# Hybrid decoder step: the products with the memory move onto units of the first output projection, the samples' rows onto score units

## Chip, core and metric

One core of a Trainium2 chip runs the whole step. The metric is the device time of one execution in microseconds (us). The kernel before takes 3266.39 us (median of three runs, 3266.05 to 3266.45).

## The reference, cut to what matters

One layer of a causal decoder runs on a prompt of 2048 tokens and on 8 samples of one token each; the width is 1024. The mixers (dilated attention and sliding-window attention) give `oa` and `ob`, which are normalised, joined and sent through `w_out`. Then comes the part that the change is about, attention to 256 memory tokens, with 4 heads of 256:

```
x = x + mixers_out(oa, ob, ...)            # ... @ w_out
k, v = split(rms_norm(mem, g_mem) @ w_mem_kv)     # memory keys and values of the prompt
q = (rms_norm(x, g_cross) @ w_xq) per head
p = softmax(q @ k.T / 16);  o = p @ v
x = x + o @ w_xo
x = x + conv_ffn(rms_norm(x, g_ffn))
```

The samples go through the same layer with memory keys and values of their own, which are inputs. All data are float32.

## The kernel before, in words

**Two halves of a product.** TensorE multiplies in a reduced float32 format, so every operand is split into a rounded part and a remainder ("hi" and "lo"; `hi_of` and `lo_of`, lines 108 to 121): ScalarE writes hi, VectorE (for some GpSimd) writes lo. Each product takes three matmuls: hi by hi, lo by hi, hi by lo.

**The weight stream.** `WStream` (line 127) holds a list of weight blocks, called units, each 512 KB, in the order in which they are used. A unit is loaded by the DMA queue of the SyncE (SP) into one of three raw tiles `wr`, split into one of four pairs `wh`, `wl`, and handed out by `get()`. `ahead(n)` writes the splits of the next n units into the program; each split also writes the loads of the next units. A unit marked whole is not split: `get_whole()` hands out the raw tile. In the kernel before the splitting stops at a whole unit until that has been handed out.

**Order of the work.** The program is written as one sequence per engine. A planner then lists each engine's instructions by a simulated time line: it keeps the written order as priority, and moves an instruction ahead where its inputs and a buffer are free. On the chip each engine, and each DMA queue, then works through its own list in order.

**The memory products.** Instead of computing queries, the kernel multiplies the weights with the memory once: for each head h, `qk_d` holds `w_xq` times the head's keys, and `vo_d` the head's values times `w_xo`. This is the block of lines 1674 to 1731, between the mixers and the output projection. For each head `mem_panel` loads keys or values (tile `kv`, split into `mkv`), `mem_q` takes a whole unit of `w_xq`, transposes it on TensorE (line 1695, 8 transposes; the result is split into `wT`) and multiplies (line 1708, 24 matmuls of 256 columns), and `mem_o` multiplies one split unit of `w_xo` (line 1721, 12 matmuls of 512 columns). Each runs twice a head. The sums lie in PSUM banks of the ring `g`, with four buffers; `store_w` copies them out (tile `az`; ScalarE for `mem_q`, VectorE for `mem_o`) and stores them to `qk_d` and `vo_d` in device memory.

**The chunks.** After that come four chunks of 512 tokens; `pre(c, ...)` (line 1282) does the part before the feed-forward, `ffn` the rest. In `pre`:
- `gemm_full(oT, ...)` multiplies the joined mixer outputs by `w_out`: 8 units, 24 matmuls of 512 columns each (lines 887 to 889); `ev_out` adds and splits each finished block.
- `scores(h)` (line 1311) multiplies by `qk_d` for head h: 2 units of 48 matmuls of 256 columns (line 1319), then the softmax; `transp` turns the softmax for the next product.
- chunk 2 takes the 8 samples along (`s_in`); after the four heads `sample_rows` (line 1357) multiplies the samples' rows, kept in `las`, by `w_xq`: 8 units of 8 matmuls of 256 columns (line 1368). Chunk 3 (`s_out`) does the same with `w_xo`, to take the samples' attention back in.
- `gemm_two` and `gemm_full` multiply by `vo_d`.

After each unit `tick()` runs one queued side task; every fourth tick issues a copy of 1 MB of the cache.

PSUM has eight banks: two in the ring `a` (`bankA`: all transposes, `sample_rows`, sums for the norms), two in `s` (scores of even heads), four in `g`.

The order of the block before `pre` is:

```
    for h in range(4):
        mk = mem_panel(h)
        for hf in range(2):
            mem_q(h, hf, mk)
        mv = mem_panel(4 + h)
        for hf in range(2):
            mem_o(h, hf, mv)
```

Of the kernel before, what the change touches and what calls it, by code (L numbers as in the profile page):

```python
# [8 lines left out]
F32 = mybir.dt.float32  # L9
# [4 lines left out]
ALU = mybir.AluOpType  # L14
# [7 lines left out]
NS = 8  # L22
# [5 lines left out]
NC = 520  # L28
# [7 lines left out]
def tile_layer(ctx: ExitStack, tc: tile.TileContext, I, C, O):  # L36
# [90 lines left out]
    class WStream:  # L127
# [11 lines left out]
            self.units.append((w, k0, nk, c0, ncol))  # L139

        def load_to(self, i):
            while self.nr <= min(i, len(self.units) - 1):
                w, k0, nk, c0, ncol = self.units[self.nr]
                t = wp.tile([128, 1024], F32, tag="wr", name=f"wr{self.nr}", bufs=self.RAW)
                self.last = dma(out=t[:, 0:nk * ncol].rearrange("p (k c) -> p k c", k=nk),
                    in_=w[k0 * 128:(k0 + nk) * 128, c0:c0 + ncol].rearrange("(k p) c -> p k c", p=128))
                self.raw[self.nr] = t
                self.nr += 1

        def split_to(self, i):  # L150
            while self.ns <= min(i, len(self.units) - 1) and self.ns not in self.whole:
                self.load_to(self.ns)
                w, k0, nk, c0, ncol = self.units[self.ns]
                n = nk * ncol
                r = self.raw.pop(self.ns)
                h = wp.tile([128, 1024], F32R, tag="wh", name=f"wh{self.ns}", bufs=self.SPL)
                l = wp.tile([128, 1024], F32R, tag="wl", name=f"wl{self.ns}", bufs=self.SPL)
                hi_of(h[:, 0:n], r[:, 0:n], "a")
                lo_of(l[:, 0:n], r[:, 0:n], h[:, 0:n], "p" if self.ns < 76 and self.ns % 2 else "v")
                self.spl[self.ns] = (h[:, 0:n].rearrange("p (k c) -> p k c", k=nk),  # L160
                                     l[:, 0:n].rearrange("p (k c) -> p k c", k=nk))
                self.ns += 1
                self.load_to(self.ns + self.RAW - 2)
# [6 lines left out]

        def get_whole(self):

            assert self.pos == self.ns and self.pos in self.whole
            self.load_to(self.pos)
            w, k0, nk, c0, ncol = self.units[self.pos]
            r = self.raw.pop(self.pos)
            self.pos += 1
            self.ns += 1
            return r[:, 0:nk * ncol].rearrange("p (k c) -> p k c", k=nk)

        def ahead(self, n):
# [32 lines left out]

    FFN_SEQ = [("up", 0), ("up", 1), ("up", 2), ("up", 3), ("up", 4), ("down", 0),
               ("up", 5), ("up", 6), ("up", 7), ("up", 8), ("down", 1), ("up", 9), ("up", 10), ("down", 2)]
    for h in range(4):
        for hf in range(2):
            W.add(w_xq, 4 * hf, 4, 256 * h, 256, whole=True)
        for hf in range(2):  # L220
            W.add(w_xo, 2 * h, 2, 512 * hf, 512)
    for c in range(4):
        add_full(w_out)
        add_full(qk_d)
        if c == 2:
            add_full(w_xq)
        if c == 3:
            add_full(w_xo)
        for mps, khs in (((0, 1), (0,)), ((0, 1), (1,)), ((2,), (0, 1)), ((3,), (0, 1))):
            for kh in khs:  # L230
                for mp in mps:
                    W.add(vo_d, 4 * kh, 4, 256 * mp, 256)
        for kind, i in FFN_SEQ:
            (add_up if kind == "up" else add_down)(i)
# [633 lines left out]
    def pieces(has_s):  # L868
        return [(0, 256), (256, NC)] if has_s else [(0, 512)]

    def gemm_b(units, panels, pcs, evac, late=None, nm=2, spare=False):

        P = {}
        nu = len(units)
        for ui, (get, pidx) in enumerate(units):
            wh, wl = get()
            for m in range(nm):
                for pi, (a, b) in enumerate(pcs):
                    if ui == 0:
                        P[m, pi] = bank("s", 2) if spare and m == 0 else bank("g", 4)  # L880
                    o = P[m, pi][:, 0:b - a]
                    for q, k in enumerate(pidx):
                        pn = panels[k]
# [12 lines left out]
            tick()  # L896

    def gemm_full(panels, pcs, evac, mps=range(4)):
        for mp in mps:
            gemm_b([(W.get, [0, 1, 2, 3]), (W.get, [4, 5, 6, 7])], panels, pcs,  # L900
                   lambda m, pi, a, b, p, mp=mp: evac(2 * mp + m, pi, a, b, p), spare=mp == 1 and len(pcs) == 2)

    class Norm:

# [377 lines left out]
    def pre(c, oT, begin):  # L1282
# [17 lines left out]
                h1[m] = split_x(x, G_CROSS, m, ncol)  # L1300
                nrm.add(x)

        gemm_full(oT, pieces(s_in), ev_out)
        del oT[:]


        p_t = {}
# [3 lines left out]
        def scores(h):  # L1311
            S = [bank("s", 2) if h % 2 == 0 else bank("g", 4) for _ in range(2)]
            for kh in range(2):
# [7 lines left out]
                               stop=(kh == 1 and q == 3 and a == 1), skip_group_check=True)  # L1321
                W.ahead(2)
                tick()
            if h == 0:
                r = sbA.tile([128, 4], F32, tag="r16", name="r16", bufs=2)
                vec.tensor_scalar(out=r, in0=nrm.r_tok()[:, 0:4], scalar1=0.0625, scalar2=None, op0=ALU.mult)
                r16.append(r)
            r = r16[0]
            out = []
# [24 lines left out]
                lo_of(pn[:, 1, 0:512], pt, pn[:, 0, 0:512])  # L1354
                pT.append(pn)

        def sample_rows(scale, done):

            row = panel32("srow")
            for mp in range(4):  # L1360
                p = bankA("t")
                for kh in range(2):
                    wh, wl = W.get()
                    for q in range(4):
                        k = 4 * kh + q
                        parts = [(p[:NS, 0:256], las[:, k, 0:NS], wl), (p[:40, 0:256], las[:, k, :], wh)]
                        for o, x, w in parts if k else reversed(parts):
                            mm(o, x, w[:, q, :], start=(k == 0 and w is wh), stop=(k == 7 and w is wh))
                    W.ahead(2)
                z = small("zx")[:NS, 0:256]  # L1370
                act(out=z, in_=p[32:32 + NS, 0:256], func=ACTF.Copy)
                o = row[:NS, 256 * mp:256 * mp + 256]
                vec.tensor_tensor(out=o, in0=p[:NS, 0:256], in1=z, op=ALU.add)
                if scale is not None:
                    vec.tensor_scalar(out=o, in0=o, scalar1=scale, scalar2=None, op0=ALU.mult)
            done(row)

        def keep_q(row):
            dma(out=qx_d, in_=row[:NS, 0:1024])
# [42 lines left out]
        for h in range(4):  # L1422
            scores(h)
            if h:
                transp(h - 1)
            if h == 0 and s_in:
                for k in range(8):
                    for i in range(2):
                        pl.tensor_copy(out=las[:, k, 32 * i:32 * i + NS], in_=h1[k][:, i, 512:NC].bitcast(F32))
        if s_in:  # L1430
            sample_rows(nrm.r[:NS, 4:5], keep_q)
        if s_out:
            sample_rows(None, add_xo)
        gemm_two(pT, ev_xo, lambda: transp(3))
        gemm_full(pT, pieces(False), ev_xo, range(2, 4))
        return h2, nrm2
# [249 lines left out]

    THREE = ((0, 0), (0, 1), (1, 0))

    def mem_q(h, hf, mk):
        w = W.get_whole()  # L1690
        T = []
        for dt in range(2):
            pt = bankA("t")
            for q in range(4):
                nc.tensor.transpose(pt[:, q * 128:(q + 1) * 128], w[:, q, dt * 128:dt * 128 + 128], ident)
            pn = panel("wT")
            hi_of(pn[:, 0, 0:512], pt, "a")
            lo_of(pn[:, 1, 0:512], pt, pn[:, 0, 0:512])
            T.append(pn)
        W.load_to(W.pos + 1)  # L1700
        W.ahead(1)
        for fp in range(2):
            p = bank("g", 4)
            for f in range(2):
                fb = 2 * fp + f
                for dt in range(2):
# [4 lines left out]
            r0 = (4 * hf + 2 * fp) * 128  # L1711
            store_w(p, "a", qk_d[r0:r0 + 256, 256 * h:256 * h + 256].rearrange("(f p) c -> p f c", p=128))

    def mem_o(h, hf, mv):
        w = W.get()
        W.ahead(1)
        for kb in range(2):
            p = bank("g", 4)
            for dt in range(2):
                for a, b in THREE:  # L1720
                    mm(p, mv[:, a, dt * 256 + kb * 128:dt * 256 + kb * 128 + 128], w[b][:, dt, :],
                       start=(dt == 0 and a + b == 0), stop=(dt == 1 and a == 1))
            store_w(p, "v", vo_d[(2 * h + kb) * 128:(2 * h + kb + 1) * 128, 512 * hf:512 * hf + 512])

    for h in range(4):
        mk = mem_panel(h)
        for hf in range(2):
            mem_q(h, hf, mk)
        mv = mem_panel(4 + h)
        for hf in range(2):  # L1730
            mem_o(h, hf, mv)
    oT = []
    for go in heads_T(0, oT):
        go()
# [74 lines left out]
```

## Time and profile before

| | us |
|---|---|
| median of three runs | 3266.39 |
| the profiled execution's own time | 3269.64 |
| its span, first to last instruction | 3267.9 |
| TensorE busy | 3103.2 (95%) |
| VectorE, ScalarE, GpSimd busy | 2123.1 (65%), 1415.6 (43%), 1017.9 (31%) |
| mean granted TensorE clock, 1 being 2.4 GHz | 0.974 |

The span is a time line on which every instruction of every engine stands with its start and its duration. The page gives each engine's busy time, first for the whole span, then in 40 slices. A matmul's duration includes the time for which it overlaps the next one, so the pace of a run of matmuls is read from start to start. The bracket behind a row of the time line is the idle time of that engine just before the row, and the instruction that ended it.

### The profile page before, as it was taken

To read this page: it belongs to the slowest core of one execution; us is meant where nothing else is said; L and a number is where in the kernel's file an instruction comes from. 1 tells how busy PE (TensorE), PEld (TensorE's weight loads), DVE (VectorE), ACT (ScalarE), POOL (GpSimd) and SP (SyncE) were. 2 spreads that over 40 slices of the span, in tenths; PEclk is the share of its full clock that TensorE was granted. 3 is DMA by queue.
4 is the path that set the end of the run, shared out by engine and by line. 5 is a ranking of instruction groups with operands and counts; after the bars stand their busy time and mean duration, and the time that the engine had idled before them with its cause. 6 is when DMAs were issued, how large, how long until landed. Compare 5 with 4: busy or idle time off the path is not lost. (4 is left out here: it accounts for less than half of the span.)

```text
span 3267.9 us, 58603 instructions
## 1 busy us (share of the span) xinstructions
PE 3103.2 (95%) x22584; PEld 2733.0 (84%) x22584; DVE 2123.1 (65%) x4209; ACT 1415.6 (43%) x2760; POOL 1017.9 (31%) x952
## 2 busy tenths in 40 slices
PE   8999989889876799999999999999999999999998
PEld 8898888888876698888888777888877778899998
DVE  7687677787874456766556767565686665555543
ACT  3456555666663344322334423444433333432322
POOL 2611513214341014643311434440464332110102
PEclk9999999998998899999999999999999999999999
DMA  6899998999897544665454454564476445322231
GB/s 210 241 258 240 260 247 232 249 240 214 194 230 222 183 149 151 201 208 194 164 189 142 157 190 153 178 206 165 151 242 229 175 140 179 122 91 91 91 95 63
DMA packets 639984, 599.06 MB, mean 183 GB/s; under 512 B 264892, under 2 KB 569192, under 8 KB 638592
## 3 DMA queue, kind: packets, MB, share of 16 engines
q1 hardware_dynamic: 634952, 591.08, 62.1%
q10 hardware_dynamic: 4608, 4.20, 0.4%
q8 instruction: 178, 2.92, 0.4%
q14 instruction: 102, 0.84, 0.1%
q0 software_dynamic: 144, 0.03, 0.0%
HBM read 466.98 MB, written 145.05 MB: 187 GB/s over the span
## 5 line engine op out<-in xcount | busy, mean ns | idle before, releaser
L121 DVE TENSOR_TENSOR wl<-wr,wh 128x1024 fp32r<-128x1024 f32 (+1 forms) x430 | 569.1, 1324 | 393.4 <-ACT wh L111 392.3
L111 ACT ACTIVATE wh<-wr 128x1024 fp32r<-128x1024 f32 x468 | 485.7, 1041 | 777.3 <-PE g L889 343.7
L888 PE MATMUL g<-h,wl 128*128 128x512 f32 (+2 forms) x1760 | 616.5, 350 | 1.4 <-DVE wl L121 1.4
L887 PE MATMUL g<-h,wh 128*128 128x512 f32 (+2 forms) x1760 | 617.2, 351 | 0.0
L889 PE MATMUL g<-h,wh 128*128 128x512 f32 (+2 forms) x1760 | 613.7, 349 | 0.0
L887 PEld LDWEIGHTS g<-h,wh 128*128 128x128 f32 x1760 | 330.8, 188 | 50.2 <-issue 0.7
L888 PEld LDWEIGHTS g<-h,wl 128*128 128x128 f32 x1760 | 330.8, 188 | 48.2 <-DVE wl L121 1.8
L889 PEld LDWEIGHTS g<-h,wh 128*128 128x128 f32 x1760 | 330.9, 188 | 47.0
L697 PE MATMUL g<-wh,xh 128*128 128x256 f32 x1152 | 342.3, 297 | 2.8 <-DVE r L256 1.3
L699 PE MATMUL g<-wh,xl 128*128 128x256 f32 x1152 | 334.3, 290 | 0.3 <-DVE xl L121 0.3
L698 PE MATMUL g<-wl,xh 128*128 128x256 f32 x1152 | 333.7, 290 | 0.0
L887 PE MATMUL g<-act,wh 128*128 128x512 f32 (+2 forms) x880 | 308.8, 351 | 1.6 <-DVE va L1512 0.9
L888 PE MATMUL g<-act,wl 128*128 128x512 f32 (+2 forms) x880 | 307.8, 350 | 0.6 <-DVE wl L121 0.6
L889 PE MATMUL g<-act,wh 128*128 128x512 f32 (+2 forms) x880 | 306.5, 349 | 0.0
L586 ACT ACTIVATE sm<-sm,ost 128x256 f32<-128x256 f32 (+1 forms) x512 | 234.8, 460 | 159.2 <-DVE ost L584 156.1
L917 POOL TENSOR_TENSOR sq<-sq 128x512 f32<-128x512 f32 (+1 forms) x83 | 125.2, 1509 | 557.1 <-ACT sq L912 555.6
L697 PEld LDWEIGHTS g<-wh,xh 128*128 128x128 f32 x1152 | 225.4, 196 | 8.1 <-DVE r L256 1.7
L699 PEld LDWEIGHTS g<-wh,xl 128*128 128x128 f32 x1152 | 224.5, 195 | 3.3 <-DVE xl L121 0.6
L698 PEld LDWEIGHTS g<-wl,xh 128*128 128x128 f32 x1152 | 225.1, 195 | 2.1 <-issue 0.2
L121 POOL TENSOR_TENSOR wl<-wr,wh 128x1024 fp32r<-128x1024 f32 x38 | 96.5, 2540 | 346.4 <-ACT wh L111 308.6
L610 PEld LDWEIGHTS <-pT 128*128 128x128 f16 x4240 | 145.7, 101 | 66.9 <-DMA pT<-p 57.1
L595 DVE TENSOR_TENSOR p<-sm,p 128x1024 f16<-128x1024 f32 (+1 forms) x128 | 151.5, 1184 | 62.3 <-ACT p L594 61.9
(388 smaller groups left out, 6785.8 us busy)
## 6 DMA issues: line engine op xcount, KB each, us to landing
wr<-in_w_up_dram SPq DMA_DIRECT2D x176, 512.0 KB
wr<-in_w_down_dram SPq DMA_DIRECT2D x80, 512.0 KB
out_dram<-in_cache_a_k_dram SPq DMA_DIRECT2D x32, 1023.5 KB
out_dram<-in_cache_a_v_dram SPq DMA_DIRECT2D x32, 1023.5 KB
wr<-in_w_in_dram SPq DMA_DIRECT2D x60, 512.0 KB
v<-va_d SPq DMA_DIRECT2D x60, 384.0 KB
wr<-in_w_out_dram SPq DMA_DIRECT2D x32, 512.0 KB
wr<-qk_d SPq DMA_DIRECT2D x32, 512.0 KB
```

The lines of the kernel that those rows point to most:

```text
L111: act(out=out, in_=in_, func=ACTF.Copy)
L121: e.tensor_tensor(out=out, in0=in_, in1=hi.bitcast(F32), op=ALU.subtract)
L586: act(out=sm[:, x, 0:n], in_=sm[:, x, 0:n], func=ACTF.Exp, scale=0.125, bias=nb[:, x:x + 1], accum_out=job.ost[:, 520 + 4 * i + x:521 + 4 ...
L595: vec.tensor_tensor(out=p2[:, 1], in0=sm[:, :, 0:n], in1=p2[:, 0], op=ALU.subtract)
L610: mm(o, p_[:, hf, x, :], v[:, g, :], start=(x == 0 and hf == 0 and n_ == 0), stop=(hf == nh - 1 and n_ == 4), skip_group_check=True)
L697: mm(p[:, 0:256], h[:, kt, :], wh[:, q, :], start=(kt == 0), stop=False)
L698: mm(p[:, 0:256], h[:, kt, :], wl[:, q, :], start=False, stop=False)
L699: mm(p[:, 0:256], l[:, kt, :], wh[:, q, :], start=False, stop=(kt == 7))
L887: mm(o, wh[:, q, c], pn[:, 0, a:b], start=st, stop=False)
L888: mm(o, wl[:, q, c], pn[:, 0, a:b], start=False, stop=False)
L889: mm(o, wh[:, q, c], pn[:, 1, a:b], start=False, stop=en)
L917: pl.tensor_tensor(out=acc[:, 0:self.ncol], in0=acc[:, 0:self.ncol], in1=sq[:, 0:self.ncol], op=ALU.add)
```

## The change

The memory products are split into three kinds of steps: T (take the whole unit and transpose it; in the first T of a head also load and split its keys and values), Q (the matmuls with the keys, and their stores) and O (the matmuls with the values, and their stores). Seven steps stand before the first chunk (T, T, Q, O, Q, O of head 0, and the first T of head 1). The others hang on the units of the first chunk's `w_out`: after each of the first six units a Q, a T and an O follow (no T after the sixth). The sums of Q and O now lie in the ring `s` (two banks) in place of `g` (four).

The samples' rows are no longer a loop of their own: in chunks 2 and 3 one of its units follows each score unit. Its sum stays in a bank of the ring `a` from one unit to the next. The copies into `las` are written before the scores, and the norm `rt` is computed after the first head's second unit, ahead of the samples' unit.

The stream's order of units follows; splitting now passes over whole units, and a load is not written while the whole unit that last had its raw tile is not handed out.

```diff
         def load_to(self, i):
-            while self.nr <= min(i, len(self.units) - 1):
+            while self.nr <= min(i, len(self.units) - 1) and self.nr - self.RAW not in self.whole:
...
         def split_to(self, i):
-            while self.ns <= min(i, len(self.units) - 1) and self.ns not in self.whole:
+            while self.ns <= min(i, len(self.units) - 1):
                 self.load_to(self.ns)
+                if self.ns in self.whole:
+                    self.ns += 1
+                    continue
+                if self.ns not in self.raw:
+                    return
...
-    for h in range(4):
-        for hf in range(2):
-            W.add(w_xq, 4 * hf, 4, 256 * h, 256, whole=True)
-        for hf in range(2):
-            W.add(w_xo, 2 * h, 2, 512 * hf, 512)
+    MP_FIRST = [("T", 0, 0), ("T", 0, 1), ("Q", 0, 0), ("O", 0, 0), ("Q", 0, 1), ("O", 0, 1), ("T", 1, 0)]
+    MP_OUT = [[("Q", 1 + u // 2, u % 2)] + ([] if u == 5 else [("T", 1 + (u + 1) // 2, (u + 1) % 2)]) +
+              [("O", 1 + u // 2, u % 2)] for u in range(6)] + [[], []]
...
+    add_mp(MP_FIRST)
     for c in range(4):
-        add_full(w_out)
-        add_full(qk_d)
-        if c == 2:
-            add_full(w_xq)
-        if c == 3:
-            add_full(w_xo)
+        for u in range(8):
+            W.add(w_out, 4 * (u % 2), 4, 256 * (u // 2), 256)
+            if c == 0:
+                add_mp(MP_OUT[u])
+        for u in range(8):
+            W.add(qk_d, 4 * (u % 2), 4, 256 * (u // 2), 256)
+            if c >= 2:
+                W.add(w_xq if c == 2 else w_xo, 4 * (u % 2), 4, 256 * (u // 2), 256)
...
     def gemm_b(...):
...
             W.ahead(2)
             tick()
+            if after:
+                after()
...
-        gemm_full(oT, pieces(s_in), ev_out)
+        gemm_full(oT, pieces(s_in), ev_out, after=(lambda: mem_steps(mp_out.popleft())) if c == 0 else None)
...
                 W.ahead(2)
                 tick()
+                if h + kh == 1 and kh == 1:
+                    rt = nrm.r_tok()
+                    srow_["r"] = rt[:NS, 4:5]
+                if c >= 2:
+                    sample_unit(h, kh)
...
-            sample_rows(nrm.r[:NS, 4:5], keep_q)
+            keep_q(srow_["row"])
         if s_out:
-            sample_rows(None, add_xo)
+            add_xo(srow_["row"])
...
-    def mem_q(h, hf, mk):
+    def mem_t(h, hf):
+        if hf == 0:
+            mkv[h] = mem_panel(h), mem_panel(4 + h)
         w = W.get_whole()
...
+        turned[h, hf] = T
         W.load_to(W.pos + 1)
-        W.ahead(1)
+
+    def mem_q(h, hf):
+        T, mk = turned.pop((h, hf)), mkv[h][0]
         for fp in range(2):
-            p = bank("g", 4)
+            p = bank("s", 2)
...
-    def mem_o(h, hf, mv):
+    def mem_o(h, hf):
         w = W.get()
-        W.ahead(1)
+        mv = mkv[h][1]
         for kb in range(2):
-            p = bank("g", 4)
+            p = bank("s", 2)
...
+        W.ahead(2)
...
+    mp_out = deque(MP_OUT)
+    W.ahead(1)
+    mem_steps(MP_FIRST)
```

## Rows read from the trace of the kernel before

**Rows 1.** The page: busy time of each engine; TensorE's tenths in 40 slices.

```profile
PE 3103.2 (95%) x22584; PEld 2733.0 (84%) x22584; DVE 2123.1 (65%) x4209; ACT 1415.6 (43%) x2760; POOL 1017.9 (31%) x952
PE   8999989889876799999999999999999999999998
```

**Rows 2.** Stretches: length, busy per engine (instructions), granted clock, DMA share, GB/s.

```profile
1006.69:1116.51 109.82, 74.11 (x371) 64.38 (x369) 41.21 (x64) 36.22 (x59) 7.26 (x6) 0.78 0.60 190
1116.51:1162.80 46.29, 46.29 (x211) 37.73 (x209) 27.88 (x30) 19.13 (x28) 8.40 (x6) 1.00 0.62 204
2213.00:2258.76 45.76, 45.76 (x392) 45.72 (x391) 22.37 (x48) 16.02 (x35) 4.23 (x4) 1.00 0.40 139
2258.76:2272.71 13.95, 10.73 (x78) 8.52 (x77) 11.51 (x22) 10.39 (x19) 0.00 (x0) 0.88 0.50 153
2803.65:2820.91 17.26, 11.47 (x83) 8.54 (x82) 12.93 (x20) 11.32 (x20) 0.00 (x0) 0.86 0.53 158
2820.91:2840.00 19.09, 19.09 (x84) 15.27 (x84) 6.65 (x8) 5.59 (x7) 1.99 (x8) 0.94 0.53 161
```

**Rows 3.** Waits, 1003 to 1118 us: total, times, longest.

```profile
ACT mkv L111 <- DMA kv<-mkv_d: 30.9, 8, 9.8
PE g L1708 <- ACT wT L111: 19.4, 5, 5.6
ACT wh L111 <- DMA wr<-in_w_xo_dram: 12.8, 7, 4.2
```

**Rows 4.** TensorE's time line in the memory products: start, duration, count, wait.

```profile
1020.20 4.08 PE L1708 MATMUL g<-mkv,wT 128*128 128x256 f32 x18 [1.62 <-ACT wT L111]
1040.50 2.50 PE L1708 MATMUL g<-mkv,wT 128*128 128x256 f32 x10 [5.35 <-ACT wT L111]
1046.92 0.60 PE L1695 MATMUL t<-ident,wr 128*128 128x128 f32 x4
1047.28 2.49 PE L1708 MATMUL g<-mkv,wT 128*128 128x256 f32 x18
1049.60 0.60 PE L1695 MATMUL t<-ident,wr 128*128 128x128 f32 x4
1058.81 0.86 PE L1721 MATMUL g<-wh,mkv 128*128 128x512 f32 x3
1059.51 0.39 PE L1721 MATMUL g<-wl,mkv 128*128 128x512 f32 x1
```

**Rows 5.** ScalarE's copies out of the products' banks: count, least, median, greatest ns.

```profile
L111 ACT ACTIVATE az<-g x16: 579/598/601, 1016.1 to 1103.6; 128x512 f32<-128x512 f32 x16
```

**Rows 6.** Time lines of the SP queue and of ScalarE: two loads and their users.

```profile
1006.78 0.42 SPq L1677 DMA_DIRECT2D kv<-mkv_d  x1
1009.81 0.63 ACT L111 ACTIVATE mkv<-kv 128x512 fp32r<-128x512 f32 x1 [2.54 <-DMA kv<-mkv_d]
1007.91 0.56 SPq L145 DMA_DIRECT2D wr<-in_w_xo_dram  x1
1014.66 1.06 ACT L111 ACTIVATE wh<-wr 128x1024 fp32r<-128x1024 f32 x1 [3.25 <-DMA wr<-in_w_xo_dram]
```

**Rows 7.** TensorE's time line, chunk 2, from the last score to `vo_d`.

```profile
2261.98 0.31 PE L1368 MATMUL t<-wh,las 128*40 128x256 f32 x1 [2.19 <-DVE pT L121]
2268.82 0.28 PE L1368 MATMUL t<-wh,las 128*40 128x256 f32 x1
2268.94 0.28 PE L1368 MATMUL t<-wl,las 128*8 128x256 f32 x1
2271.29 0.28 PE L1368 MATMUL t<-wl,las 128*8 128x256 f32 x1 [1.04 <-DVE wl L121]
2273.97 0.50 PE L1413 MATMUL g<-pT,wl 128*128 128x512 f32 x1 [0.53 <-DVE wl L121]
```

**Rows 8.** The same of chunk 3.

```profile
2806.86 0.31 PE L1368 MATMUL t<-wh,las 128*40 128x256 f32 x1 [2.18 <-DVE pT L121]
2818.18 1.22 PE L1412 MATMUL g<-pT,wh 128*128 128x512 f32 x2 [3.23 <-ACT wh L111]
```

More of the change, by code (lines that the diff above doesn't have):

```diff
@@ L171, in get_whole @@
         def get_whole(self):
-            assert self.pos == self.ns and self.pos in self.whole
             self.load_to(self.pos)
@@ L176, in get_whole @@
             r = self.raw.pop(self.pos)
+            self.whole.remove(self.pos)
             self.pos += 1
-            self.ns += 1
+            self.ns = max(self.ns, self.pos)
             return r[:, 0:nk * ncol].rearrange("p (k c) -> p k c", k=nk)
@@ L216, in tile_layer, with add_mp @@
                ("up", 5), ("up", 6), ("up", 7), ("up", 8), ("down", 1), ("up", 9), ("up", 10), ("down", 2)]
-    for h in range(4):
-        for hf in range(2):
-            W.add(w_xq, 4 * hf, 4, 256 * h, 256, whole=True)
-        for hf in range(2):
-            W.add(w_xo, 2 * h, 2, 512 * hf, 512)
-    for c in range(4):
-        add_full(w_out)
-        add_full(qk_d)
-        if c == 2:
-            add_full(w_xq)
-        if c == 3:
-            add_full(w_xo)
+    MP_FIRST = [("T", 0, 0), ("T", 0, 1), ("Q", 0, 0), ("O", 0, 0), ("Q", 0, 1), ("O", 0, 1), ("T", 1, 0)]
+    MP_OUT = [[("Q", 1 + u // 2, u % 2)] + ([] if u == 5 else [("T", 1 + (u + 1) // 2, (u + 1) % 2)]) +
+              [("O", 1 + u // 2, u % 2)] for u in range(6)] + [[], []]
+    def add_mp(steps):
+        for kind, h, hf in steps:
+            if kind == "T":
+                W.add(w_xq, 4 * hf, 4, 256 * h, 256, whole=True)
+            elif kind == "O":
+                W.add(w_xo, 2 * h, 2, 512 * hf, 512)
+    add_mp(MP_FIRST)
+    for c in range(4):
+        for u in range(8):
[6 more added lines that the diff above has]
+                W.add(w_xq if c == 2 else w_xo, 4 * (u % 2), 4, 256 * (u // 2), 256)
         for mps, khs in (((0, 1), (0,)), ((0, 1), (1,)), ((2,), (0, 1)), ((3,), (0, 1))):
@@ L869, in pieces, with gemm_b @@
         return [(0, 256), (256, NC)] if has_s else [(0, 512)]
-    def gemm_b(units, panels, pcs, evac, late=None, nm=2, spare=False):
+    def gemm_b(units, panels, pcs, evac, late=None, nm=2, spare=False, after=None):
         P = {}
@@ L896, in gemm_b, with gemm_full @@
             tick()
-    def gemm_full(panels, pcs, evac, mps=range(4)):
+            if after:
+                after()
+    def gemm_full(panels, pcs, evac, mps=range(4), after=None):
         for mp in mps:
             gemm_b([(W.get, [0, 1, 2, 3]), (W.get, [4, 5, 6, 7])], panels, pcs,
-                   lambda m, pi, a, b, p, mp=mp: evac(2 * mp + m, pi, a, b, p), spare=mp == 1 and len(pcs) == 2)
+                   lambda m, pi, a, b, p, mp=mp: evac(2 * mp + m, pi, a, b, p), spare=mp == 1 and len(pcs) == 2,
+                   after=after)
     class Norm:
@@ L1301, in ev_out @@
                 nrm.add(x)
-        gemm_full(oT, pieces(s_in), ev_out)
+        gemm_full(oT, pieces(s_in), ev_out, after=(lambda: mem_steps(mp_out.popleft())) if c == 0 else None)
         del oT[:]
+        if s_in:
+            for k in range(8):
+                for i in range(2):
+                    pl.tensor_copy(out=las[:, k, 32 * i:32 * i + NS], in_=h1[k][:, i, 512:NC].bitcast(F32))
         p_t = {}
@@ L1323, in scores @@
                 tick()
+                if h + kh == 1 and kh == 1:
[3 more added lines that the diff above has]
+                    sample_unit(h, kh)
             if h == 0:
                 r = sbA.tile([128, 4], F32, tag="r16", name="r16", bufs=2)
-                vec.tensor_scalar(out=r, in0=nrm.r_tok()[:, 0:4], scalar1=0.0625, scalar2=None, op0=ALU.mult)
+                vec.tensor_scalar(out=r, in0=rt[:, 0:4], scalar1=0.0625, scalar2=None, op0=ALU.mult)
                 r16.append(r)
@@ L1355, in transp, with sample_unit @@
                 pT.append(pn)
[L1357 to L1369, printed above, removed]
+        srow_ = {}
+        def sample_unit(mp, kh):
+            if kh == 0:
+                srow_["p"] = bankA("t")
+                if mp == 0:
+                    srow_["row"] = panel32("srow")
+            p, row = srow_["p"], srow_["row"]
+            wh, wl = W.get()
+            for q in range(4):
+                k = 4 * kh + q
+                parts = [(p[:NS, 0:256], las[:, k, 0:NS], wl), (p[:40, 0:256], las[:, k, :], wh)]
+                for o, x, w in parts if k else reversed(parts):
+                    mm(o, x, w[:, q, :], start=(k == 0 and w is wh), stop=(k == 7 and w is wh))
+            W.ahead(2)
+            if kh:
                 z = small("zx")[:NS, 0:256]
@@ L1373, in sample_rows @@
                 vec.tensor_tensor(out=o, in0=p[:NS, 0:256], in1=z, op=ALU.add)
-                if scale is not None:
-                    vec.tensor_scalar(out=o, in0=o, scalar1=scale, scalar2=None, op0=ALU.mult)
-            done(row)
+                if s_in:
+                    vec.tensor_scalar(out=o, in0=o, scalar1=srow_["r"], scalar2=None, op0=ALU.mult)
         def keep_q(row):
@@ L1425, in pre @@
                 transp(h - 1)
[L1426 to L1429, printed above, removed]
         if s_in:
-            sample_rows(nrm.r[:NS, 4:5], keep_q)
+            keep_q(srow_["row"])
         if s_out:
-            sample_rows(None, add_xo)
+            add_xo(srow_["row"])
         gemm_two(pT, ev_xo, lambda: transp(3))
@@ L1687, in tile_layer @@
     THREE = ((0, 0), (0, 1), (1, 0))
-    def mem_q(h, hf, mk):
+    mkv, turned = {}, {}
+    def mem_t(h, hf):
+        if hf == 0:
+            mkv[h] = mem_panel(h), mem_panel(4 + h)
         w = W.get_whole()
@@ L1723, in mem_o, with mem_steps @@
             store_w(p, "v", vo_d[(2 * h + kb) * 128:(2 * h + kb + 1) * 128, 512 * hf:512 * hf + 512])
[L1725 to L1731, printed above, removed]
+        if hf:
+            mkv.pop(h)
+        W.ahead(2)
+    def mem_steps(steps):
+        for kind, h, hf in steps:
+            {"T": mem_t, "Q": mem_q, "O": mem_o}[kind](h, hf)
+    mp_out = deque(MP_OUT)
+    W.ahead(1)
+    mem_steps(MP_FIRST)
     oT = []
```

## The prediction, made before the changed kernel was run

> **What bounds the kernel now.** I read the page first: TensorE is busy 95% of the span and no other engine over 65%, and among the 40 slices TensorE's row dips only where the mixers give way to the memory products, a third of the way in [rows 1]. So time comes back only where TensorE waits, or runs slowly, and all that is taken off its queue there reaches the end. Next I cut the span into stretches [rows 2]. The reader is to see two kinds. In the first `w_out` (46.29 us) and in a chunk's scores (45.76 us) TensorE is busy throughout at granted clock 1.00. In the memory products (109.82 us) it is busy 74.11 us at a mean clock of 0.78, and the two loops of the samples' rows (13.95 and 17.26 us) are alike, with 0.88 and 0.86. The change lays work of the second kind on work of the first.
>
> The table of waits says why the products are slow [rows 3]: ScalarE waits 30.9 us for the keys and values to load, TensorE 19.4 us for the transposed weights that ScalarE copies behind them. Each head is a chain of load, split, transpose, copy, multiply, with nothing else to do meanwhile. The clock is its second half: the 18 matmuls from 1020.20 take 3.88 us up to the last start, 0.216 us each, those from 1047.28 take 0.129 us each [rows 4]. The pace of the first group is that of 1.2 GHz, and it stands behind a wait.
>
> **The products: what they cost by themselves.** From start to start [rows 4]: four transposes take 1047.28 - 1046.92 = 0.36 us, 0.09 each; the 18 matmuls of 256 columns to the next row 2.32 us, 0.129 each; three of 512 columns 0.70 us, 0.233 each. So a T of 8 costs 0.72 us, a Q of 24 3.10 us, an O of 12 2.80 us. Eight of each are 52.9 us. With 16 transposes for `w_out`'s operand, also done in that stretch (1.4 us), 55.5 of the 109.82 us are waiting and half rate. That is all that this part can give.
>
> **The seven steps in front.** Nothing lets them start earlier: the first keys are issued at 1006.78 and ScalarE has them at 1009.81 [rows 6], so the first Q starts where it does now, near 1011, 4.3 us into the stretch. Behind it are two T, two Q, two O (13.2 us) and the 16 operand transposes (1.4 us), which no longer fall into gaps: 14.6 us. The values now load beside the keys rather than after the Qs, which takes out the wait ahead of the first O. I keep one group at half rate (18 matmuls at 0.216 rather than 0.129 us, 1.6 us, doubled because the first Q too comes behind a wait: 3.2 us) and two waits as long as the one at 1020.20 (1.62 us each). `w_out` starts at 1011 + 14.6 + 3.2 + 3.2 = 1032.
>
> **The steps on `w_out`.** Its 192 matmuls and 16 more transposes take the 46.29 us of now [rows 2]. Added are six Q, five T and six O: 18.6 + 3.6 + 16.8 = 39.0 us. Without a wait the stage ends at 1032 + 46.3 + 39.0 = 1117.3; it ends at 1162.80 now. Is there cover? Per inserted step TensorE has 5.6 us of `w_out` and 6.5 us of products.
> - ScalarE and VectorE: both stretches together hold 55.35 and 69.09 us of their work, against 111 us of new stage, 50% and 62% [rows 2].
> - DMA: 0.60 x 109.82 + 0.62 x 46.29 = 94.6 us of its time, 85% of 111 us. In the six full steps it is closer: 1.57 MB of units, 1.05 MB of stores, 0.26 MB of keys and values, and some 0.8 MB of residual tiles and cache copies per step are 3.7 MB in 12.1 us, 305 GB/s, while 190 GB/s at share 0.60 and 204 at 0.62 [rows 2] mean 317 to 329 GB/s for a full share. This is the thinnest cover.
> - Latency: a unit issued at 1007.91 was split from 1014.66, 6.75 us with other loads beside it [rows 6]. The stream holds three raw tiles, here one each for `w_out`, `w_xq` and `w_xo`, and each comes round once in 12.1 us; 6.75 us fits, some 12 would not.
> - Banks: the sums have two banks rather than four. ScalarE's copy out takes 0.60 us [rows 5], the other bank fills for 1.5 us, so TensorE waits only where the copy is queued behind something: behind a split whose unit has not landed.
>
> Per full step the wait lies between 0 and what the products have now behind a late load, 5.35 us [rows 4]. I take 1.3 us, a quarter, near the short row of 1.62 us: 8 us in all. The stage ends at 1125, 37.7 us earlier. With a wait of 0 it would be 46, with 5.35 us in each step and no slow clock 14.
>
> A bank wait is also where a rule weighs against the change. The Trainium skill (Perfetto Trace Analysis, Optimizing Tensor Performance, Matmuls) says that independent groups of matmuls should rotate through different PSUM banks, so that copying one out overlaps the next. By that rule, taken to its end, each of the 24 groups left on `w_out` would wait out a copy; the row gives 0.60 us a copy, so 14 us rather than part of 8. I go by the rows, in which a bank's copy is shorter than the other's filling.
>
> **The samples' rows.** A matmul of their loops follows the last in 0.12 us (2268.82 to 2268.94) [rows 7], so 64 take 7.5 us; they stay on TensorE. Now they run in a row, eight units in some 10 us, and wait for the transposes' copies (2.19 and 2.18 us), the splits (1.04 and 0.53 us) [rows 7] and in chunk 3 the first split of `vo_d` (3.23 us) [rows 8].
> - Chunk 2: 13.95 + 0.53 = 14.5 us from the last score until `vo_d` runs freely. Left are 7.5 us, 12 transposes (1.1 us) and 0.5 us of wait for a bank of ring `a`: 9.1. Gain 5.4 us.
> - Chunk 3: 17.26 us, of which 0.46 us is `vo_d`'s, and in the stretch behind it a clock of 0.94 for 19.09 us, so 1.1 us lost. Left are 9.4 us with the small transposes. Gain 8.5 us.
>
> The cover in the scores is wide: DMA share 0.40, ScalarE 16.02 and VectorE 22.37 of 45.76 us [rows 2], to which eight splits add 8.5 us on ScalarE (1.06 us each [rows 6]); VectorE's half, even at twice that, 17 us, would still fit. If a sample unit's split is late, TensorE waits ahead of the next score unit: between 0 and 1.04 us each [rows 7]; I take 0, since a score unit lasts 5.7 us. The copies into `las` and the norm's earlier place cost nothing: GpSimd is busy 31% [rows 1], and the first samples' unit follows a score unit that needs the same blocks. Uncovered they would be one wait of 2 to 3 us.
>
> **The sum.** 37.7 + 5.4 + 8.5 = 51.6 us, off the profiled execution's 3269.64: 3218.0. The median of the runs lies 3.25 us below that execution, so 3214.8.
>
> **The rivals.**
> - *The steps wait each time* (loads late, ScalarE's queue blocked, two banks). For it: the thin DMA cover, and 12.8 us that ScalarE already waits for units in seven splits [rows 3]. Against it: `w_out` and the products have each a third of every 12.1 us to themselves. At 5.35 us a step, without slow clock, the products give 14 and the samples 13.9: 3238.5.
> - *The change doesn't do what it says*: the planner, free to move what is ready, runs `w_out`'s matmuls ahead of steps whose operands it thinks late, and leaves a tail of products by themselves. For it: it already moves transposes between other heads' matmuls [rows 4]. Against it: it keeps the written order as priority. With half of the six steps exposed at the present cost, some 19 of the 37.7 us are left: 3233.
> - *Half rate, the slower side.* Late splits, one mechanism: ScalarE stands at a split whose unit has not landed, TensorE waits, and the granted clock falls to 1.2 GHz as it does behind such waits now. The price is 5.35 us for the wait and, if the next 6.8 us run at half rate, 3.4 us more: 8.75 us in each of six steps, 52.5 us in place of my 8, and 1.04 us at each of the 16 samples' units, 16.6 us. That is 61.1 us more than forecast: 3276, slower than before. It decides from 8 + 51.6 = 59.6 us over 22 inserted units on, 2.7 us for each. Against it: none of the two covering stretches shows a wait or a clock below 1.00 [rows 2].
>   The Trainium skill (TensorE: Matmul & The Clock Gate, HAM oscillation) describes this case: matmul bursts separated by waits for DMA start cold each time. The 0.78 of the products agrees, and it is what the rule would make of every step.
>
> **How the numbers follow.** The forecast (waits of 0 to 2.6 us a step, so 3207 to 3223, with the front some 4 us either way 3203 to 3227) has 0.62. The waiting steps have 0.18, the planner's order 0.08, half rate 0.06; 0.06 is for all that falls together to about nothing. What a measurement of this kernel can tell from no change is 0.2%, 6.5 us. Faster by more takes the first three: 0.88; the same 0.05; slower 0.07. The range reaches over the first two rivals' times and, below, over no waits at all with a quick front (51.6 + 8 + 6): 3200 to 3240.
>
> **What would show it.** In the trace after: the last `w_out` matmul of chunk 0 near 1125, six groups of T, Q and O between its units; a granted clock of 1.00 there; the rows of waits for `kv` under 10 us; no stretch with the samples' matmuls alone, and `vo_d` directly behind the last score. Wrong would be: a DMA share over 0.9 with TensorE idle behind `wh` or `az` copies (first rival), products after the last `w_out` unit (second), a clock under 0.9 on `w_out` (third).

## The result, and the profile after

The changed kernel takes 3222.47 us (median of 4 runs, 3214.29 to 3232.28), the kernel before 3266.22 us beside it (4 runs, 3262.1 to 3266.45): ratio 0.987, 95% interval 0.9841 to 0.9899. That is 43.8 us less, where 51.6 were forecast. The profiled execution of after is the slowest of its four, 3232.28 us with a span of 3230.5, so the stages are compared from mark to mark within each trace and not by the span.

The page of the kernel after, its rows for those of [rows 1]: the busy time of each engine, and TensorE's tenths in 40 slices.

```profile
PE 3089.1 (96%) x22584; PEld 2721.3 (84%) x22584; DVE 2125.9 (66%) x4209; ACT 1417.2 (44%) x2760; POOL 1017.4 (31%) x952
PE   8999899889886999999999999999999999999999
```

The instructions are the same in number. Of the dip (7 6 7 in three slices before) one 6 is left. The samples' rows, whose loops are much shorter than a slice, show in neither row.

Next the stretches of after, with the columns of [rows 2]: from the first transpose of the products to the first `w_out` matmul; from there to the first score; then, for chunks 2 and 3, from the first score to the first `vo_d` matmul.

```profile
1009.35:1049.97 40.62, 23.89 (x128) 21.10 (x127) 18.80 (x34) 16.64 (x28) 7.26 (x6) 0.73 0.70 227
1049.97:1138.14 88.17, 85.11 (x453) 71.51 (x451) 44.57 (x59) 39.00 (x59) 8.61 (x5) 0.98 0.69 229
2189.51:2245.51 56.00, 56.00 (x480) 54.95 (x479) 34.56 (x66) 27.33 (x50) 6.03 (x7) 1.00 0.54 178
2729.23:2784.93 55.70, 55.70 (x477) 54.72 (x476) 33.85 (x62) 28.60 (x51) 3.62 (x3) 1.00 0.45 141
```

The covered parts are nearly dense: 3.06 us idle in 88.17, none in the samples' two. The part in front, up to `w_out`, is not: TensorE is busy for 23.89 of 40.62 us at a mean clock of 0.73, no better than the old products stage at 0.78 [rows 2]. From first transpose to first score it is 128.8 us, 156.2 before: a gain of 27.4 where 37.7 were forecast.

The table of waits of after from 1005 to 1140 us (total, times, longest) answers to [rows 3].

```profile
ACT wh L111 <- DMA wr<-in_w_xo_dram: 24.1, 8, 5.3
PE s L1741 <- ACT wT L111: 13.1, 2, 8.6
ACT mkv L111 <- DMA kv<-mkv_d: 6.4, 7, 2.2
PE s L1754 <- ACT az L111: 4.0, 3, 1.8
PE s L1741 <- DVE az L115: 1.4, 1, 1.4
```

The wait for keys and values fell from 30.9 to 6.4 us, but TensorE still waits 13.1 us for `wT` copies, 8.6 of them at once, and ScalarE's wait for `w_xo` units has doubled, from 12.8 to 24.1. The time line around that one wait tells how they hang together (start, duration, engine, what; in brackets the idle time before it and what ended it).

```profile
1023.93 0.60 PE L1725 MATMUL t<-ident,wr 128*128 128x128 f32 x4
1035.06 0.37 SPq L145 DMA_DIRECT2D wr<-in_w_xo_dram  x1
1035.66 0.33 SPq L1711 DMA_DIRECT2D vo_d<-az  x1
1036.04 0.43 SPq L1703 DMA_DIRECT2D kv<-mkv_d  x1
1036.73 0.32 SPq L1711 DMA_DIRECT2D vo_d<-az  x1
1037.10 0.45 SPq L1703 DMA_DIRECT2D kv<-mkv_d  x1
1040.91 1.06 ACT L111 ACTIVATE wh<-wr 128x1024 fp32r<-128x1024 f32 x1 [5.29 <-DMA wr<-in_w_xo_dram]
1042.17 0.63 ACT L111 ACTIVATE mkv<-kv 128x512 fp32r<-128x512 f32 x1 [0.21 <-DMA kv<-mkv_d]
1043.42 0.63 ACT L111 ACTIVATE mkv<-kv 128x512 fp32r<-128x512 f32 x1 [0.62 <-DMA kv<-mkv_d]
1043.96 1.06 ACT L111 ACTIVATE wT<-t 128x512 fp32r<-128x512 f32 x2
1044.59 1.22 PE L1741 MATMUL s<-mkv,wT 128*128 128x256 f32 x4 [8.61 <-ACT wT L111]
```

To be read upward from the last row. The third T's transposes were done by 1024.5; their copy stands on ScalarE at 1043.96, behind the splits of head 1's keys and values, which stand behind the split of a `w_xo` unit. SP issued the keys at 1036.04 and the values at 1037.10, among the last stores of head 0: the keys behind one `vo_d` store and ahead of the other. It issued the unit at 1035.06, right behind the end (1035.04) of the VectorE split that freed a raw tile. Until the copy both banks of ring `a` are full, so the transposes of `w_out`'s operand can't run either, and `w_out`, which needs nothing of the products, waits with them. TensorE's idle stretch by itself, with the columns of [rows 2]:

```profile
1035.98:1044.59 8.61, 0.00 (x0) 0.00 (x0) 3.02 (x4) 2.85 (x5) 0.63 (x1) 0.63 0.57 192
```

### The profile page after: what moved, and what is told of

The parts are those of the page before. It is cut to its first block, busy times and chain, and to the rows that moved or that the text cites. A ratio compares the mean times of both kernels' runs of the same rounds, so it can differ in the third digit from the quotient of the medians.

```text
span 3230.5 us, 58603 instructions
## 1 busy us (share of the span) xinstructions
PE 3089.1 (96%) x22584; PEld 2721.3 (84%) x22584; DVE 2125.9 (66%) x4209; ACT 1417.2 (44%) x2760; POOL 1017.4 (31%) x952
## 4 chain that ended last, share of the span: by engine, by line
PE 61%; DMA 8%; DVE 8%; POOL 3%; issue 3%; ACT 2%; SPq 1%; POOLq 0%; DVEq 0%; ACTq 0%
PE g L903 14%; PE g L904 14%; PE g L902 14%; DMA pT<-p 4%; PE g L1341 3%; PE s L1341 3%; DVE wl L121 2%; PE o L625 1%; DMA mrg<-o_d 1%; PE g L712 1%; PE g L713 1%; PE g L714 1%; POOL mrg L1033 1%; PE se L588 1%; DVE p L610 1%
## 5 line engine op out<-in xcount | busy, mean ns | idle before, releaser
L902 PEld LDWEIGHTS g<-act,wh 128*128 128x128 f32 x880 | 165.2, 188 | 28.1 <-issue 2.5
```

## The experiments

The mixers' end, from which the products start, lay anywhere from 995.9 to 1009.4 us in the twelve profiles, with the same code ahead of it. So besides the medians I give for every run the time from first transpose (T) to first `w_out` matmul and to first score.

| kernel | median us (runs) | ratio to before, 95% | T to `w_out` | T to score |
|---|---|---|---|---|
| change, again (e0_again) | 3221.60 (5) | 0.9865, 0.9846 to 0.9883 | 40.57 | 127.50 |
| products alone (e1_products) | 3233.63 (6) | 0.9908, 0.9893 to 0.9924 | 41.02 | 129.00 |
| samples alone (e2_samples) | 3250.56 (6) | 0.9954, 0.9940 to 0.9968 | 108.81 | 155.22 |
| head 1's keys early (e3_kv_early) | 3210.21 (4) | 0.9828, 0.9811 to 0.9846 | 18.86 | 114.48 |
| the same, again (e3_again) | 3208.73 (4) | 0.9831, 0.9817 to 0.9845 | 18.83 | 114.75 |
| their loads early, not the splits (e8_kv_loads) | 3209.95 (5) | 0.9825, 0.9809 to 0.9840 | 18.11 | 114.78 |
| eight units (e4_eight) | 3212.89 (5) | 0.9832, 0.9813 to 0.9851 | 16.00 | 113.19 |
| eight units, keys early (e6_eight_kv) | 3209.11 (4) | 0.9825, 0.9811 to 0.9838 | 16.77 | 108.41 |
| meant for one bank (e5_one_bank) | 3208.47 (4) | 0.9829, 0.9814 to 0.9844 | 18.98 | 114.32 |
| one bank (e7_one_bank) | 3226.70 (4) | 0.9879, 0.9858 to 0.9900 | 19.22 | 128.26 |

My theory after the first result: the two coverings work, what is missing lies in the front, and there it is the place of head 1's loads in SP's order. The rivals: the steps or the samples' units pay their missing part themselves; the front is short of DMA or of clock, whatever its order; the two banks cost it.

**The change again, and each half alone.** No edit in the first; in the second the samples' loops are those of before, in the third the products and the stream.

```diff
 e1_products
-            if c >= 2:
-                W.add(w_xq if c == 2 else w_xo, 4 * (u % 2), 4, 256 * (u // 2), 256)
+        if c >= 2:
+            add_full(w_xq if c == 2 else w_xo)
...
 e2_samples
-            if c == 0:
-                add_mp(MP_OUT[u])
...
```

> The changed kernel as it is, for a second profile and its spread. Theory 'front': what is missing of the forecast lies between the first T and the first matmul of w_out, 40.6 us in the profile at hand (1009.35 to 1049.97) where 26 were forecast, and hangs on when loads land; so runs differ by some 10 us or more, and in a faster execution this stretch is shorter by about what the whole is. Median 3215 to 3227. Rival 'samples or mixers': the stretch is as long in both profiles and the runs differ elsewhere.

> The products on w_out alone; the samples' rows stay a loop of their own, as before. Profile of the change: products gave 27 us in an execution of 3232 us, the samples' rows 6.2 and 9.6. Theory 'two parts that add': 15 us slower than the change in the same rounds, 3229 to 3241 against 3266. Rival 'the samples' rows give nothing by themselves' (what they save comes back as a wait elsewhere): the same as the change, about 3222.

> The samples' rows on score units alone; the products stay in front of the chunks, as before. Theory 'two parts that add': 15 us faster than before, 3248 to 3254, with little spread. Rival: within 5 us of before. The sum of both parts' gains should be that of the change within the spread.

Against the 3266.29 us of before beside them, the change gains 44.7 us, the products alone 32.7, the samples alone 15.7: together 48.4, additive within the spread of the runs. From T to score, though, the products alone gain 27.2 us (156.2 to 129.0), so some 5 of their 32.7 lie outside the stage. The stretches of the two halves are those of the change. Products alone: front and rest of the products' stage, then chunk 2 from its last score to `vo_d`.

```profile
1000.94:1041.96 41.02, 22.99 (x128) 20.32 (x127) 18.43 (x34) 16.59 (x28) 7.37 (x6) 0.75 0.70 225
1041.96:1129.94 87.98, 84.08 (x453) 70.26 (x451) 45.46 (x59) 38.98 (x59) 8.78 (x5) 1.00 0.70 229
2228.17:2242.71 14.54, 10.82 (x78) 8.23 (x75) 11.52 (x22) 10.30 (x19) 0.00 (x0) 0.88 0.49 148
```

Samples alone: first transpose to first `w_out` matmul, then chunk 2 from first score to `vo_d`.

```profile
1000.58:1109.39 108.81, 72.21 (x370) 63.30 (x369) 41.23 (x64) 36.31 (x59) 6.24 (x6) 0.80 0.59 191
2205.38:2261.37 55.99, 55.99 (x481) 54.99 (x479) 34.57 (x66) 27.31 (x50) 6.02 (x7) 1.00 0.53 177
```

Each half has its own stage as the change has it and leaves the other as it was. The missing 8 us are not in the samples, and not in a quarrel between the halves; the front of 41 us is there with the products alone. It also has nearly the same length in three executions (40.62, 40.57, 41.02), so the runs' spread of some 18 us is not the front's, as I first thought; the two profiles of the change differ by 5.9 us in span, of which 3.2 lie ahead of the first T.

**Head 1's keys and values early.** In e3 load and split, in e8 the load alone, right behind the first two T.

```diff
 e3_kv_early
-        if hf == 0:
+        if hf == 0 and h != 1:
             mkv[h] = mem_panel(h), mem_panel(4 + h)
...
         turned[h, hf] = T
+        if (h, hf) == (0, 1):
+            mkv[1] = mem_panel(1), mem_panel(5)
...
 e8_kv_loads: mem_load(j) issues the DMA of mem_panel(j)
         turned[h, hf] = T
+        if (h, hf) == (0, 1):
+            mem_load(1)
+            mem_load(5)
```

> As the change, but the keys and values of head 1 are loaded and split right after the first two T, before the first Q, not behind O of head 0. Theory 'front, by the SP queue's order': in the profile of the change these loads were issued at 1036.04 and 1037.10, behind stores, ScalarE split them from 1042.17, and TensorE waited 8.6 us for the wT copies behind them; with early loads w_out starts some 8 us sooner, and the time is 6 to 10 us below the change, 3212 to 3217. Rival 'late units': ScalarE stands at splits of w_xo (5.3 us ahead of 1040.91) whatever the keys do; then the 8.6 us shrink by 3 at most and the time is within 3 us of the change. Rival 'banks': TensorE waits for az copies; no change either.

> The same kernel as e3_kv_early, run beside the next three so that they share a chip. Expected: 3204 to 3215 us, ratio 0.981 to 0.985, and 113 to 116 us from the first transpose of the products to the first score. If the 11 us below the change were an accident of one chip or one execution, it would lie near 3221 here, with 127 to 129 us.

> The change with only the loads of head 1's keys and values issued early, right behind the first two T; their splits stay where they are in the change, at the head of the third T (in e3_kv_early both were early). If the place of the loads in SP's queue is what costs the front, most of e3's 11 to 13 us come back: 19 to 32 us from the first transpose to the first matmul of the output projection, 115 to 122 to the first score, 3208 to 3216. If it is ScalarE's order (it stands at a late split of a unit while both transpose banks wait for it, whether or not the keys have landed): 35 to 41 us, 124 to 129 us, 3217 to 3227.

e3 lies 11.4 us below the change, more than the 6 to 10 expected, and 13 below it from T to score; repeated on another chip it is the same. Its stretches in the second profile, with the row of its loads:

```profile
998.99:1017.82 18.83, 13.79 (x82) 12.73 (x81) 11.74 (x25) 10.13 (x18) 0.00 (x0) 0.73 0.92 304
1017.82:1113.74 95.92, 91.89 (x499) 76.32 (x497) 51.08 (x69) 44.10 (x68) 15.03 (x12) 1.00 0.76 251
1000.21 1.52 SPq L1703 DMA_DIRECT2D kv<-mkv_d  x3
```

The loads now go out by 1001.7, 2.7 us behind the first T rather than 28; `w_out` begins after 18.83 us, and the rest of the stage carries more of the products at full clock. The wait of 8.61 us is not there. The DMA share in front rises to 0.92, and still the front is short; in the change it was 0.70, and 0.57 during the wait of 8.61 us. So it was not DMA that the change's front lacked.

e8 was to tell SP's order from ScalarE's, and does so only in part. Its loads are early and its splits written where the change has them, but the planner moved these too; the time line of ScalarE in e8 has head 1's two splits at

```profile
1010.26 1.14 ACT L111 ACTIVATE mkv<-kv 128x512 fp32r<-128x512 f32 x2
```

So e8's front runs in the order of e3's, from another program text. What it shows is that the written place of the loads is enough: with the loads early the planner also put the splits forward, and in e3 and e8 the third T's copies (1012.60 and 1012.25) stand ahead of the next `w_xo` split. What either queue alone, SP's or ScalarE's, would have delayed stays open: in the change ScalarE stood 5.29 us at the `w_xo` unit, which was not held up by the keys. Nor is it shown why the planner put the loads so late. In the change it moved the keys ahead of one store only of those written before them. The keys, values and `az` copies also share the seven buffers of `small`, and no run parts the order of the queue from the buffers.

**Eight units instead of six.** Only the first two T stay in front, the other steps go behind all eight `w_out` units; in e6 the keys and values of each next head are also loaded behind the second T of the head before.

```diff
-    MP_FIRST = [("T", 0, 0), ("T", 0, 1), ("Q", 0, 0), ("O", 0, 0), ("Q", 0, 1), ("O", 0, 1), ("T", 1, 0)]
...
+    MP_FIRST = [("T", 0, 0), ("T", 0, 1)]
+    MP_OUT = [[("Q", u // 2, u % 2), ("O", u // 2, u % 2)] + ([] if u > 5 else [("T", (u + 2) // 2, u % 2)]) for u in range(8)]
```

> The change with only the two transpose steps of head 0 in front and the Q, O and T steps spread over all eight units of the first output projection; the loads of keys and values stay at the head of each T step, as in the change. Theory one (what is left in front is paid in waits and at half rate, and the projection covers it): 104 to 112 us from first transpose to first score, and the time at or below that of e3_kv_early, 3200 to 3210. Theory two (keys and values of every next head are again issued behind two stores of the head before, and ScalarE stands at a late split with both transpose banks full, now for heads 1, 2 and 3): waits of 5 to 9 us per head come back, 118 to 130 us, 3215 to 3225.

> e4_eight with the keys and values of each next head loaded and split right behind the transposes of the head before. If the order of SP's queue is what delays the products, this has no wait over 2 us on a transposed weight: 103 to 110 us from first transpose to first score, 3199 to 3207, and below e4_eight by what e4_eight waits for its wT copies. If it is not, e4_eight and this are alike within 3 us.

Neither beats e3: 3212.9 and 3209.1 against 3208.7 on the same chip, their intervals one over the other. e4 first, then e6 with a third stretch, from first score to `vo_d`:

```profile
1006.50:1022.50 16.00, 11.44 (x62) 10.15 (x61) 8.58 (x21) 7.99 (x14) 2.42 (x3) 0.68 0.82 273
1022.50:1119.69 97.19, 92.12 (x505) 78.25 (x504) 55.77 (x73) 45.92 (x72) 14.03 (x10) 0.98 0.74 234
```

```profile
1004.70:1021.47 16.77, 11.39 (x62) 10.04 (x61) 9.04 (x20) 8.92 (x16) 0.00 (x0) 0.69 0.90 286
1021.47:1113.12 91.65, 90.25 (x506) 76.53 (x504) 55.16 (x75) 46.17 (x71) 14.49 (x12) 1.00 0.79 260
1113.12:1165.00 51.88, 51.88 (x430) 51.33 (x429) 24.60 (x49) 18.27 (x38) 4.07 (x3) 1.00 0.46 155
```

e4 idles 5.07 us from its first `w_out` matmul to the first score, e6 1.40. Both theories of e4 miss: its idle time there is mostly waits for `az` copies (3.8 us) and for VectorE's split of `wT` (1.2), not waits of 5 to 9 us per head for the keys, and its 113.19 us lie above the one range and below the other. As e4 has no wait left for ScalarE's `wT` copies behind its first Q, what e6 gains over it is not shown to come from early keys. From T to score e6 is 6.3 us better than e3, but the last O now lies between the scores, which take 51.88 rather than 48.81 us, so 3.3 us are left up to `vo_d`. e3, its repeat, e5 and e8 agree within 0.5 us there, but the medians show nothing of the 3.3. The first 16 to 19 us stay at a clock of about 0.7 in e3, e4, e6 and e8 (0.68 to 0.73), whatever stands there: in each the first Q waits 4.5 to 5.3 us for the `wT` copies, which stand behind the first keys and values on ScalarE.

**One bank instead of two**, on e3. The first edit asks for a bank and leaves it empty; the second holds one from the first Q to the last O.

```diff
 e5_one_bank
+            bank("s", 2)
             p = bank("s", 2)
...
 e7_one_bank
+            if (kind, h, hf) == ("Q", 0, 0):
+                kept.append(bank("s", 2))
+                nc.tensor.transpose(kept[0][:, 0:128], ident, ident)
             {"T": mem_t, "Q": mem_q, "O": mem_o}[kind](h, hf)
+            if (kind, h, hf) == ("O", 3, 1):
+                act(out=small("az")[:, 0:128], in_=kept.pop()[:, 0:128], func=ACTF.Copy)
```

> e3_kv_early with the sums of Q and O in one bank rather than two (every second turn of the ring is left empty), the computation unchanged. If TensorE waits out a copy at every group when there is no other bank, the 32 groups pay 0.6 us and more each, 19 to 30 us: 3230 to 3240, and 134 to 145 us from first transpose to first score. If the planned order puts matmuls of the output projection between the groups, the copy is covered: 0 to 6 us, 3205 to 3217, and 114 to 121 us. That tells what a second bank is worth here, and so whether two banks rather than four could have cost the change anything.

> e3_kv_early with one of the two banks of the sums taken out of use from the first Q to the last O (a transpose of the identity is held in it), so that every sum of Q and O goes into the same bank; in e5_one_bank the trace shows both still in use. If TensorE waits out a copy at every group when there is no other bank, the 32 groups pay 0.6 us and more each, 19 to 30 us: 3228 to 3240, and 134 to 145 us from first transpose to first score. If the planned order puts matmuls of the output projection between the groups, which in e3_kv_early already lie between most of them, only the pairs of Q groups that follow each other at once pay, 8 of them at some 1 us and a few more where the copy is late: 5 to 15 us, 3214 to 3224, and 119 to 130 us.

e5 says nothing of banks: an empty tile takes none, and in its trace groups still start before the copy of the group ahead has begun. It is in effect a third run of e3. e7 has one bank; its time line, at a pair of Qs:

```profile
1061.28 1.68 PE L1743 MATMUL s<-mkv,wT 128*128 128x256 f32 x12 [1.62 <-DVE az L115]
1062.99 0.60 ACT L111 ACTIVATE az<-s 128x512 f32<-128x512 f32 x1 [2.59 <-PE s L1743]
1063.64 1.67 PE L1743 MATMUL s<-mkv,wT 128*128 128x256 f32 x12 [0.69 <-ACT az L111]
1065.35 0.60 ACT L111 ACTIVATE az<-s 128x512 f32<-128x512 f32 x1 [0.24 <-PE s L1743]
```

Matmuls 1.68 us, copy 0.60 as in [rows 5], and 0.05 us behind its end the next group. It costs 18.0 us over e3's repeat in the medians and 16.8 over e8, which ran beside it on the same chip: above the 5 to 15 expected and under the 19 of every group waiting. T to `vo_d` gives 18.0, 181.56 us against 163.56. Only part of it are waits for `az` copies, 8.0 us where e3's repeat has 2.7. In e7 transposes also wait 5.5 us for VectorE's split of `wT` and `w_out` 3.9 us for split units (none and 0.8 in e3's repeat), and TensorE is busy 4.3 us longer. The order has changed too: the last three groups lie among chunk 0's scores, which begin at 1124.18 while the last O ends at 1138.23. That the planner spread them to avoid the copies is likely, but not shown.

## Why the prediction was nearly right

The median came 7.7 us above the forecast and well within its range, by the mechanism forecast. By its steps:

- *What bounds the kernel.* Right: both covered stretches are dense, with the clock at 0.98 to 1.00, and the gain lies there. (The 3.88 us that I read from 1020.20 in [rows 4] run to the start of the next row, at 1024.08, and not to the last start; the pace of 0.216 us stands.)
- *The seven steps in front.* This term failed, and it is the miss. `w_out` was to start 25.3 us behind the first T; it was 40.62. After the first Q I had allowed "two waits as long as the one at 1020.20 (1.62 us each)"; the idle stretches there are 1.41, 0.76, 1.44 and 8.61 us, 9.0 us more than my 3.2. The first Q itself came 2.1 us later than I put it (rows below), and the planner put one Q of the covered part into the front (3.1 us) and left half of the operand transposes behind (0.7), 2.4 us net. Of the 15.3 us that leaves 1.8, put down to half rate. I had asked whether the first keys can come earlier and not where the *second* head's keys stand in SP's order: in the seventh step of the front, among head 0's last stores. Writing those two loads earlier brings T to score to 114.5 to 114.8 us (e3, e8), below the forecast of 118.3. The 2.1 us are a price of loading the values beside the keys, which I had counted as a gain alone: ScalarE now waits 1.77 us for the values and splits them ahead of the first `wT` copies, which come 5.81 us behind the first T; in the kernel before they came 3.66 us behind it (1010.35 and 1006.69).

```profile
1014.62 0.63 ACT L111 ACTIVATE mkv<-kv 128x512 fp32r<-128x512 f32 x1 [1.77 <-DMA kv<-mkv_d]
1015.16 1.07 ACT L111 ACTIVATE wT<-t 128x512 fp32r<-128x512 f32 x2
```

- *The steps on `w_out`.* Right, and better than the 8 us of waits: 88.17 us from first `w_out` matmul to first score with 3.06 idle, where 93 were forecast with 2.4 us more of work. The DMA share, the cover that I thought thinnest, is 0.69 there.
- *The samples' rows.* Right with a size slightly off: up to `vo_d` chunk 2 gained 6.2 us (62.20 to 56.00; 5.4 forecast), chunk 3 7.1, and 2.4 more up to the first `up` matmul where the clock had sagged before (8.5 forecast in all). No sample unit made TensorE wait, and none of the waits of [rows 7, 8] is left.
- *The sum.* 27.4 and 15.8 make 43.2; the medians gave 43.8 and 44.7. That they agree within 1.5 us is partly luck: from the first T to the end of the span the two profiles of the change are 40.0 and 42.8 us shorter than that of before, and ahead of the first T executions differ by up to 13.5 us.
- *The rivals.* Waits in every step: no, 3.06 us idle in the whole stage. Half rate: in front, and once on `w_out`, where the granted clock in the change's profile is 0.50 (1.2 GHz) for 3.42 us from 1103.13, behind a wait of 1.77 us for an `az` copy; in e0_again's profile that stretch has 1.00 throughout. The planner leaving a tail of products: not in the change, but with one bank (e7) it does; with eight units (e4, e6) the last steps are written behind the last `w_out` unit.
- *The rule on banks.* The Trainium skill (Perfetto Trace Analysis, Optimizing Tensor Performance, Matmuls) would have groups rotate through different banks. With two, TensorE waits 5.4 us for the copies in the change (4.0 and 1.4 in the table of waits); with one, on e3, 17 to 18 us more are lost. So the trace agrees for the second bank. What a third would give was not run.

Among the signs that I had named, the waits for `kv` (6.4 us) and the samples inside the scores came true; the last `w_out` matmul near 1125 did not: it started at 1137.9, by the front's excess.

What stays open: whether the queues' order or the buffers held head 1's keys back, why the mixers' stage varies from execution to execution, and what e6 would be worth if its last steps lay ahead of the scores.

## What to carry to other kernels

When work is laid onto another stage, look at what is left alone in front of it: here one late wait, of 8.6 us, was most of the miss. Write loads ahead of the stores of the step before, not at the head of the step that uses them; 13 of the 42 us that the products give in e3 (156.2 to 114.5) hung on the written place of two loads. A second bank for sums was worth 17 to 18 us here, though TensorE's waits for copies without it were only 8: part of a shortage shows as other waits and another order.

The Trainium skill (Perfetto Trace Analysis, DMA Optimizations) says that it may pay to give loads and stores an issuing engine each. The trace of the change shows such a case, a load at 1036.04 behind a store at 1035.66 on one queue; no run here tries a second queue, and an earlier place in the same one was enough.

## What the runs showed that was not expected

- The same code ahead of the products ended 13.5 us apart in twelve profiles (995.9 to 1009.4). Span less first T is steadier: 2221.2 and 2218.4 us in two profiles of the change whose spans differ by 5.9 (3230.5 and 3224.6), 2206.7 and 2207.7 in two of e3 (3202.6 and 3206.7), 2204.2 in e5. A stage is best measured from a mark beside it.
- Loading the values beside the keys delays the first Q: it starts 5.4 to 7.2 us behind the first T in the ten profiles with the products moved, and 4.3 and 4.1 in before and e2. No run splits the values later.
- With one bank a group of sums starts 0.05 us behind the end of the copy ahead of it, so a pair of groups is 2.36 us apart (1061.28 to 1063.64) rather than 1.6.
